# Up projection of a hybrid decoder step: products paired within each token half, six weight pairs in plain form for the first half, norms cut into small steps

## The chip, the cores and the metric

The kernel runs on one core of a Trainium2 chip. The metric is the device time of one execution in microseconds (us). TensorE (PE in the profile) multiplies matrices, VectorE (DVE), ScalarE (ACT) and GpSimd (POOL) work element by element, SyncE (SP) starts transfers between HBM and the on-chip memory SBUF. A product lands in one of eight PSUM banks, and another engine reads it from there.

## The reference

One layer of a decoder for 1024 prompt tokens and 8 sequences of 4 decode tokens, 1056 tokens in all. Two mixing branches run side by side (attention with a forget gate, and a chunkwise mLSTM); their merged output goes through an output projection, two RMS norms with the residual between, and a squared-ReLU MLP. Cut to what lies behind the mixing:

```python
y  = merged @ w_out                                  # 1024 x 1024
x1 = x + gt_m * rmsnorm(y, g_post_mix)
h  = rmsnorm(x1, g_pre_mlp) * (1 + sc_f) + sh_f
u  = jnp.square(jax.nn.relu(h @ w_up))               # w_up 1024 x 4096
x2 = x1 + gt_f * rmsnorm(u @ w_down, g_post_mlp)     # w_down 4096 x 1024
```

Here `sc`, `sh`, `gt` are vectors of a conditioning input, one for the prompt and one for each decode sequence, so the 32 decode columns need factors of their own. They are the last columns of the second token half.

## The kernel before

Activations lie transposed: 128 features on the partitions, tokens along the row. A feature tile (ft) is 128 features; 1024 features are eight of them. Tokens are cut into two halves of 528 (`th` 0 and 1), each into two chunks of 264 (`TQ`).

Each float32 product is made of three matmuls in a faster format. An operand is split into a high part (a cast on ScalarE, `ph`) and a low part (the rest, by a subtraction, `pl`); hi·hi, hi·lo and lo·hi are summed. `split4` does this for a weight of 128x512 (L1237, L1239): every third subtraction goes to VectorE, the others to GpSimd.

*Output projection* (`wout`). For each token half, feature tile and chunk, 24 matmuls go to one of three PSUM banks named `g` (L1386 to L1388). VectorE copies the bank out (L1391), ScalarE squares it, GpSimd adds up the squares (L1397).

*Norms* (`norms(th)`). A generator that is carried on at fixed places. It turns the sums of squares into a scale (`rstd`, L1266 to L1268: small matmuls on TensorE, one step on VectorE, one on GpSimd), spreads it over the partitions by small matmuls (L1279) and, for all eight feature tiles, scales (L1290), adds the residual (L1349), sums squares anew (L1355); then a second `rstd`, a second scaling and a shift on ScalarE (L1365). It has four places to pause. `NORM_AT` lists at which tiles of the second half's output projection a piece of the first half's norm is issued; `NORM2_AT` does it for the second half's norm during the first products of the up projection.

*Up projection*. Weights are taken in pairs of feature tiles, sixteen pairs. Each pair is a 2x2 block product in seven products for eight (Winograd's form). The two block rows of the activations are feature tiles 0-3 and 4-7; the two block columns are the token halves 0 and 1. So the operands (`T1` to `T4`, sums and differences, made and split into hi and lo by `operands`, L1414 to L1426) need both halves. While the second half's norm runs, `first_two` does the two of the seven products that need the first half alone for six pairs (`PRE`), and writes one of them to HBM (`d_s`) for later; ScalarE and VectorE empty its banks (L1463, L1467). After that `operands()` is issued in one go, then `pair` sixteen times, with weight sums `S` on VectorE (L1475 to L1478). Products go to banks named g, s, t and o. Results are squared-ReLU'd on ScalarE (L1449, L1450) and written to HBM (`d_u`).

*Down projection*. Eight blocks `j` of four feature tiles of u. `load_u` (L1563 to L1565) reads them back from HBM and splits them; it stands behind the last pair. There are eight buffers of each part, so two blocks are loaded ahead. Each block multiplies with 32 pieces of w_down (loaded as `raw`, L1230, in three buffers) and adds to accumulators. In the tail come the last norm, transposes and the output's transfers; their tiles use the same eight buffers.

The order on every engine comes from the order in which the program issues instructions, and a scheduler of the framework that works with modelled times. `after(last.ins)` ties a piece to the place behind a given matmul. Every engine runs its own list in order.

Of the kernel before, what the change touches and what calls it, by code (L numbers as in the profile page):

```python
# [18 lines left out]
P = 128  # L19
# [50 lines left out]
def hybrid_kernel(ctx: ExitStack, tc: tile.TileContext, ins, outs):  # L70
# [1112 lines left out]
    ms2 = ExitStack()  # L1183
    mgp = ms2.enter_context(tc.tile_pool(name="mg", bufs=1, reuse_waits="tile", side="right"))
# [9 lines left out]
    MG = [(tl(mgp, [P, 8, TQ], F32R, "X", 8), tl(mgp, [P, 8, TQ], F32R, "X", 8)) for _ in CQ]  # L1194
# [54 lines left out]
    d_s = tl(dr, [PRE, P, TH], F32, "d_s")  # L1249
# [86 lines left out]

    def norms(th):
# [20 lines left out]
        yield  # L1358
# [3 lines left out]
        for ft in range(8):  # L1362
            y = Y(th, ft)
            scaled(y, r2, a_f, ft, m, TH)
            act.activation(y[:, :m], y[:, :m], AF.Identity, bias=sh_f[:, ft, 0:1])  # L1365
            if m < TH:
                per_seq(y, y, sh_f, ft, m, TH, ALU.add)
            if th == 0 and ft % 4 == 3:
                part(ft // 4, Q[0][ft // 4], qp, mgp)
        yield  # L1370

    xTs, turns = {}, {}
    chain = iter(())
    for th in range(2):
        a = th * TH
        Q.append([xs(qp, F32) for _ in range(2)])
        ssq = ssqs[th] = sums(npl, TH)
        for fp in range(4):
            wr = raw_w(w_out, 0, 8, fp * 2 * P, 2 * P)
            for ft in (2 * fp, 2 * fp + 1):  # L1380
                pieces = [split4(wr[:, 4 * kh:4 * kh + 4, (ft % 2) * P:(ft % 2 + 1) * P]) for kh in range(2)]
                for si, (a_, b_) in enumerate(CQ[2 * th:2 * th + 2]):
                    o = bank("g")[:, :TQ]
# [14 lines left out]
                    with after(last.ins):  # L1398
                        if (ft, si) in NORM_AT:
                            next(chain, None)  # L1400
                        if si and ft in XT_AT:
                            if th not in turns:
                                xTs[th] = [xs(mgp if th else qp, F32) for _ in range(2)]
                                turns[th] = turn_x(th)
                            next(turns[th], None)
        for _ in chain:
            pass
        for _ in turns[th]:
            pass
        chain = norms(th)  # L1410
    _mark(nc, "up")


    def operands():  # L1414

        (B11, B21), (B12, B22) = Q
        t3 = xs(qp, F32)
        pool.tensor_tensor(t3, B22, B12, ALU.subtract)
        dve.tensor_tensor(B12, B12, B11, ALU.subtract)
        dve.tensor_tensor(B11, B22, B12, ALU.subtract)  # L1420
        dve.tensor_tensor(B21, B21, B11, ALU.subtract)
# [6 lines left out]
    bank_n = [0]

    def bank8(which="gggsstto"):  # L1430

        bank_n[0] += 1
        return bank(which[bank_n[0] % len(which)])

    SUB = ((0, TQ), (TQ, TH))

    def product(accs_, w, x, first):

        wh, wl = w
        for (s0, s1), acc in zip(SUB, accs_):  # L1440
            o = acc[:, :TQ]
            for k in range(4):
                pe.matmul(o, wh[:, k], hi[x][:, k, s0:s1], start=first and k == 0, stop=False, skip_group_check=True)  # L1443
                pe.matmul(o, wh[:, k], lo[x][:, k, s0:s1], start=False, stop=False, skip_group_check=True)  # L1444
                last = pe.matmul(o, wl[:, k], hi[x][:, k, s0:s1], start=False, stop=k == 3, skip_group_check=True)  # L1445
        return last.ins

    def u_out(c, ft, th):
        act.activation(c, c, AF.Relu)  # L1449
        act.activation(c, c, AF.Square)  # L1450
        sp.dma_start(d_u[ft, :, th * TH:(th + 1) * TH], c)

    def first_two(i, n_):

        wr = raw_w(w_up, 0, 8, 2 * i * P, P)
        A11, A12 = split4(wr[:, 0:4]), split4(wr[:, 4:8])
        ab, bb = [bank8("gggtt") for _ in SUB], [bank8("gggtt") for _ in SUB]
        s = tl(npl, [P, TH], F32, "n", 8)
        c11 = tl(npl, [P, TH], F32, "n", 8)
        last = product(ab, A11, 0, True)  # L1460
        step(last, 2 * n_)
        for (s0, s1), acc in zip(SUB, ab):
            act.copy(s[:, s0:s1], acc[:, :TQ])  # L1463
        last = product(bb, A12, 1, True)
        step(last, 2 * n_ + 1)
        for (s0, s1), acc in zip(SUB, bb):
            dve.tensor_tensor(c11[:, s0:s1], acc[:, :TQ], s[:, s0:s1], ALU.add)  # L1467
        u_out(c11, 2 * i, 0)
        sp.dma_start(d_s[n_], s)

    def pair(i, pre):
# [7 lines left out]
        ab = [bank8() for _ in SUB]  # L1479
        tiles = {}  # L1480
        if pre:
            s = tl(npl, [P, TH], F32, "n", 8)
            sp.dma_start(s, d_s[i])

        def read(what):

            for n_, ((s0, s1), acc) in enumerate(zip(SUB, ab)):
                t = tl(npl, [P, TQ], F32, "v", 4)
                tiles[what, n_] = t
                if pre:  # L1490
                    dve.tensor_tensor(t, acc[:, :TQ], s[:, s0:s1], ALU.add)
                else:
                    act.copy(t, acc[:, :TQ])

        def add(c, what, bb):
            for n_, ((s0, s1), acc) in enumerate(zip(SUB, bb)):
                dve.tensor_tensor(c[:, s0:s1], acc[:, :TQ], tiles[what, n_], ALU.add)

        quad = lambda: tl(npl, [P, TH], F32, "n", 8)
        if not pre:  # L1500
            product(ab, split4(a11), 0, True)
            read("M1")
            bb = [bank8() for _ in SUB]
            product(bb, split4(a12), 1, True)
            c11 = quad()
            add(c11, "M1", bb)
            u_out(c11, 2 * i, 0)
# [5 lines left out]
        read("U3")
        c22 = quad()
        add(c22, "U3", db)
        u_out(c22, 2 * i + 1, 1)
        product(ab, split4(a22), "T4", False)
        c21 = quad()
        for (s0, s1), acc in zip(SUB, ab):
            if pre:  # L1520
                dve.tensor_tensor(c21[:, s0:s1], acc[:, :TQ], s[:, s0:s1], ALU.add)
            else:
                act.copy(c21[:, s0:s1], acc[:, :TQ])
# [6 lines left out]
    def step(last, at):  # L1530
        if at in NORM2_AT:
            with after(last):
                next(chain, None)
# [178 lines left out]
```

## Time and profile before

| | us |
|---|---|
| median of 3 runs | 1930.47 (1926.7 to 1931.01) |
| the profiled execution | 1938.06 |
| its span, first to last instruction | 1936.4 |
| TensorE busy | 1835.9 (95%) |
| VectorE, ScalarE, GpSimd busy | 933.3, 847.0, 498.4 |

The stages that the change touches begin at 1083.0 us of the span (second half of the output projection), 1158.9 (up projection) and 1527.9 (down projection, up to the tail at 1907.9). Matmuls overlap in the trace: one of 264 columns shows 0.28 us, while the next starts 0.12 later. The distance of the starts is what counts.

### The profile page before, as it was taken

To read this page: it belongs to the slowest core of one execution; us is meant where nothing else is said; L and a number is where in the kernel's file an instruction comes from. 1 tells how busy PE (TensorE), PEld (TensorE's weight loads), DVE (VectorE), ACT (ScalarE), POOL (GpSimd) and SP (SyncE) were. 2 spreads that over 40 slices of the span, in tenths; PEclk is the share of its full clock that TensorE was granted. 3 is DMA by queue.
4 is the path that set the end of the run, shared out by engine and by line. 5 is a ranking of instruction groups with operands and counts; after the bars stand their busy time and mean duration, and the time that the engine had idled before them with its cause. 6 is when DMAs were issued, how large, how long until landed. Compare 5 with 4: busy or idle time off the path is not lost.

```text
span 1936.4 us, 31063 instructions
## 1 busy us (share of the span) xinstructions
PE 1835.9 (95%) x12353; PEld 1727.2 (89%) x12353; DVE 933.3 (48%) x1951; ACT 847.0 (44%) x1509; POOL 498.4 (26%) x436
## 2 busy tenths in 40 slices
PE   6899999999999999999998976799999899999998
PEld 3889789898888999989898976799999799999997
DVE  3654545554445565544463446853332324343536
ACT  4646545566555444433123454545555532121212
POOL 3200010000233121101155554322223423222213
PEclk9999989999999999999999988899999899999999
DMA  8321432123556222263234324244333422222213
GB/s 269 77 68 60 142 84 78 45 82 96 175 171 212 88 55 63 70 201 114 66 96 156 123 82 148 95 141 131 95 98 119 173 89 89 95 105 89 89 42 138
DMA packets 182600, 213.37 MB, mean 110 GB/s; under 512 B 14132, under 2 KB 142704, under 8 KB 182456
## 3 DMA queue, kind: packets, MB, share of 16 engines
q1 hardware_dynamic: 177368, 194.43, 31.4%
q0 software_dynamic: 4864, 16.91, 2.6%
q8 instruction: 97, 1.59, 0.3%
q14 instruction: 47, 0.39, 0.1%
q10 hardware_dynamic: 224, 0.06, 0.0%
HBM read 166.08 MB, written 45.29 MB: 109 GB/s over the span
## 4 chain that ended last, share of the span: by engine, by line
PE 87%; DVE 4%; DMA 4%; issue 1%; ACT 1%; POOL 1%; SPq 1%; DVEq 0%; POOLq 0%; ACTq 0%
PE ps_g L408 17%; PE ps_g L410 17%; PE ps_g L409 17%; PE ps_g L1444 2%; PE ps_g L1443 2%; PE ps_g L1445 2%; PE ps_s L684 2%; PE ps_t L709 2%; PE ps_g L1386 2%; PE ps_g L1387 2%; PE ps_g L1388 2%; PE ps_t L1444 1%; PE ps_t L1445 1%; PE ps_t L1443 1%; PE ps_s L681 1%
## 5 line engine op out<-in xcount | busy, mean ns | idle before, releaser
L408 PE MATMUL ps_g<-Xh,wh 128*128 128x352 f32 (+1 forms) x1176 | 394.3, 336 | 1.2 <-ACT wh L269 1.0
L410 PE MATMUL ps_g<-Xh,wl 128*128 128x352 f32 (+1 forms) x1176 | 390.9, 334 | 0.0
L409 PE MATMUL ps_g<-Xl,wh 128*128 128x352 f32 (+1 forms) x1080 | 356.5, 330 | 0.6 <-DVE Xl L351 0.6
L408 PEld LDWEIGHTS ps_g<-Xh,wh 128*128 128x128 f32 (+1 forms) x1176 | 223.4, 190 | 7.4 <-issue 3.0
L410 PEld LDWEIGHTS ps_g<-Xh,wl 128*128 128x128 f32 (+1 forms) x1176 | 222.4, 189 | 6.2 <-issue 4.5
L408 PE MATMUL ps_g<-uh,ph 128*128 128x352 f32 x672 | 217.7, 325 | 8.1 <-ACT uh L1564 8.1
L409 PE MATMUL ps_g<-ul,ph 128*128 128x352 f32 x672 | 216.8, 323 | 1.3 <-POOL ul L1565 1.3
L410 PE MATMUL ps_g<-uh,pl 128*128 128x352 f32 x672 | 216.4, 322 | 0.0
L409 PEld LDWEIGHTS ps_g<-Xl,wh 128*128 128x128 f32 (+1 forms) x1080 | 203.9, 189 | 6.8 <-issue 3.9
L1239 POOL TENSOR_TENSOR pl<-raw,ph 128x512 fp32r<-128x512 f32 x92 | 126.9, 1381 | 280.5 <-ACT ph L1237 275.0
L1237 ACT CAST ph<-raw 128x512 fp32r<-128x512 f32 x136 | 84.0, 621 | 263.1 <-PE ps_g L409 178.6
L270 POOL TENSOR_TENSOR wl<-wr,wh 128x1024 fp32r<-128x1024 f32 x26 | 63.2, 2429 | 442.7 <-ACT wh L269 293.9
L1580 DVE TENSOR_TENSOR acc<-acc,ps_g 128x352 f32<-128x352 f32 x144 | 74.0, 519 | 163.3 <-PE ps_g L410 163.3
L408 PEld LDWEIGHTS ps_g<-uh,ph 128*128 128x128 f32 x672 | 126.8, 189 | 9.3 <-ACT uh L1564 8.3
L409 PEld LDWEIGHTS ps_g<-ul,ph 128*128 128x128 f32 x672 | 127.1, 189 | 1.7 <-POOL ul L1565 1.7
L410 PEld LDWEIGHTS ps_g<-uh,pl 128*128 128x128 f32 x672 | 126.8, 189 | 0.0
L1443 PE MATMUL ps_g<-X,ph 128*128 128x264 f32 x376 | 108.4, 289 | 12.1 <-ACT X L1311 12.1
L1444 PE MATMUL ps_g<-X,ph 128*128 128x264 f32 x376 | 108.8, 290 | 0.5 <-DVE X L1312 0.5
L1445 PE MATMUL ps_g<-X,pl 128*128 128x264 f32 x376 | 108.2, 288 | 0.0
L1386 PE MATMUL ps_g<-X,ph 128*128 128x264 f32 x256 | 77.4, 302 | 19.2 <-DVE X L1391 13.3
L1239 POOL TENSOR_TENSOR pl<-S,ph 128x512 fp32r<-128x512 f32 x42 | 57.4, 1368 | 141.1 <-ACT ph L1237 141.1
L269 ACT CAST wh<-wr 128x1024 fp32r<-128x1024 f32 x52 | 54.5, 1047 | 75.7 <-PE ps_g L409 55.0
(618 smaller groups left out, 4496.2 us busy)
## 6 DMA issues: line engine op xcount, KB each, us to landing
wr<-in_w_in SPq DMA_DIRECT2D x44, 512.0 KB
d_u<-n SPq DMA_DIRECT2D x64, 264.0 KB
ul<-d_u SPq DMA_DIRECT2D x32, 528.0 KB
wr<-in_w_ada SPq DMA_DIRECT2D x32, 512.0 KB
raw<-in_w_up SPq DMA_DIRECT2D x16, 1024.0 KB
raw<-in_w_down SPq DMA_DIRECT2D x16, 1024.0 KB
d_sg<-sgo SPq DMA_DIRECT2D x60, 176.0 KB
raw<-in_w_out SPq DMA_DIRECT2D x8, 1024.0 KB
```

Of the source, the lines that this page charges most:

```text
L269: act.copy(wh, wr)
L270: (dve if lo_turn[0] % 2 else pool).tensor_sub(wl, wr, f(wh))
L408: pe.matmul(o, wh[:, k], rh(k, a, b), start=(k == 0), stop=False)
L409: pe.matmul(o, wh[:, k], rl(k, a, b), start=False, stop=False)
L410: last = pe.matmul(o, wl[:, k], rh(k, a, b), start=False, stop=(k == nk - 1))
L1237: act.copy(h_, src)
L1239: (dve if turn[0] % 3 == 0 else pool).tensor_sub(l_, src, f(h_))
L1386: pe.matmul(o, wh[:, kk], mg_h(k, a_, b_), start=(k == 0), stop=False)
L1443: pe.matmul(o, wh[:, k], hi[x][:, k, s0:s1], start=first and k == 0, stop=False, skip_group_check=True)
L1444: pe.matmul(o, wh[:, k], lo[x][:, k, s0:s1], start=False, stop=False, skip_group_check=True)
L1445: last = pe.matmul(o, wl[:, k], hi[x][:, k, s0:s1], start=False, stop=k == 3, skip_group_check=True)
L1580: dve.tensor_tensor(accs[a // 352](ft), accs[a // 352](ft), o, ALU.add)
```

## The change

- The 2x2 block product now lies within one token half: the block columns are the half's two chunks of 264 tokens. Each half has operands of its own (`operands(th)`), of 128x1056, in named places (`AT`).
- The first six pairs are done for the first half alone in plain form (`plain`: eight block products, 96 matmuls a pair), then pairs 6 to 15 for both halves (168 each), then pairs 0 to 5 for the second half alone (84 each). `d_s` is gone.
- `norms` pauses after each feature tile and `operands` after each one or two operands: 46 steps, spread by two tables (`AT_OUT` with 21 over the 16 tiles of the second half's output projection, `AT_UP` with 25 over the 24 tiles of the plain products). The second half's residual tiles (`x_tile(1)`) move from the output projection into the plain products. Decode columns of four feature tiles are scaled by one instruction.
- The output projection and the plain products use five banks in turn (`g`, `g`, `t`, `g`, `t`). In `plain` ScalarE empties the bank with its ReLU, and all splits' subtractions go to GpSimd.
- In a pair, one of the two squared ReLUs is one step on VectorE.
- The down projection takes the blocks in the order 3 to 7, 0 to 2. Its first activations are loaded and split during the second half's pairs, into places `R0` to `R3`; those of later blocks have four buffers a block in alternation, and the tail's tiles have four for eight.

```diff
-NORM_AT = ((0, 0), (0, 1), (2, 1), (3, 1), (4, 0), (4, 1))
-NORM2_AT = (0, 1, 4, 5, 6, 7)
+AT_OUT = (1, 1, 2, 1, 2, 1, 1, 0, 1, 2, 2, 2, 2, 1, 1, 1)
+AT_UP = ((3, 1), (2, 2), *((0, n) for n in (1, 1, 2, 1, ...)))
...
-    def split4(src):
+    def split4(src, every=3):
...
-        (dve if turn[0] % 3 == 0 else pool).tensor_sub(l_, src, f(h_))
+        (dve if turn[0] % every == 0 else pool).tensor_sub(l_, src, f(h_))
...
         for ft in range(8):
             y = Y(th, ft)
-            scaled(y, r, gt_m, ft, m, TH)
+            if ft % 4 == 0 and m < TH:
+                scaled_s(Q[th][ft // 4], r, gt_m, ft // 4, m)
+            scaled_p(y, r, gt_m, ft, m)
             (pool if ft % 2 else dve).tensor_tensor(y, y, xT[ft // 4][:, ft % 4], ALU.add)
...
-        yield
+            yield
         rt = rstd(ssq2, TH)
...
+    def blocks(th):
+        return [Q[th][k][:, :, c * TQ:(c + 1) * TQ] for k in range(2) for c in range(2)]
+    def operands(th):
+        B11, B12, B21, B22 = blocks(th)
+        part(th, "B11", B11, at["B11"])
+        part(th, "B21", B21, at["B21"])
         yield
+        if th == 0:
+            part(th, "B12", B12, at["B12"])
+            part(th, "B22", B22, at["B22"])
+            yield
+        pool.tensor_tensor(t3, B22, B12, ALU.subtract)
+        dve.tensor_tensor(B12, B12, B11, ALU.subtract)
+        dve.tensor_tensor(B11, B22, B12, ALU.subtract)
+        dve.tensor_tensor(B21, B21, B11, ALU.subtract)
+        yield
+        part(th, "T2", B11, at["T2"])
+        part(th, "T1", B12, at["T1"])
+        yield
...
-                    o = bank("g")[:, :TQ]
+                    o = bank8("ggtgt")[:, :TQ]
...
-                        if (ft, si) in NORM_AT:
-                            next(chain, None)
+                        if th:
+                            steps(AT_OUT[2 * ft + si])
...
+    def plain(i, anchors):
+        for s_ in range(2):
+            pieces = [split4(wr[:, 4 * kh:4 * kh + 4, s_ * P:(s_ + 1) * P], every=99) for kh in range(2)]
+            for n_ in range(2):
+                o = bank8("ggtgt")[:, :TQ]
+                for k in range(8):
+                    (wh, wl), x, kk = pieces[k // 4], (0, f"B{k // 4 + 1}{n_ + 1}"), k % 4
+                    pe.matmul(o, wh[:, kk], hi[x][:, kk], start=(k == 0), stop=False)
+                    pe.matmul(o, wh[:, kk], lo[x][:, kk], start=False, stop=False)
+                    last = pe.matmul(o, wl[:, kk], hi[x][:, kk], start=False, stop=(k == 7))
+                act.activation(c[:, n_ * TQ:(n_ + 1) * TQ], o, AF.Relu)
...
+                with after(last.ins):
+                    at = next(anchors)
+                    for _ in range(at[0]):
+                        x_tile(1)
+                    steps(at[1])
...
+            dve.scalar_tensor_tensor(c, c, 0.0, c, ALU.max, ALU.mult)
...
+    chain = itertools.chain(chain, norms(1), operands(1))
     for i in range(PRE):
-        first_two(i, i)
+        plain(i, anchors)
     for _ in chain:
         pass
-    operands()
-    for i in range(FF // (2 * P)):
-        pair(i, i < PRE)
+    for i in range(PRE, FF // (2 * P)):
+        pair(i, (0, 1))
...
+    JS = [*range((PRE + 1) // 2, NJ), *range((PRE + 1) // 2)]
...
+            if n_ == 0:
+                t = tl(mgp, [P, 2, T], F32R, f"R{i}", 1)
+                ht, lt = t[:, 0], t[:, 1]
+            else:
+                ht, lt = (tl(dnp, [P, T], F32R, x + "ab"[n_ % 2], FC) for x in ("uh", "ul"))
...
+    for i in range(PRE):
+        pair(i, (1,))
+        if i == 1:
+            u_0 = load_u(0)
...
-            yt = tl(dnp, [P, T], F32, "ul", 8)[:, :D]
+            yt = tl(dnp, [P, T], F32, "ula", FC)[:, :D]
```

The order of instructions shows three places. First TensorE in the second half of the output projection, where the norm's second scale is made (L1266 sums, L1279 spreads it, both lines are the same in the two kernels). Before, one product stands between the two:

```order
L1386 MATMUL ps_g_11468<-X_9710,ph_11464 128x264
L1387 MATMUL ps_g_11468<-X_9711,ph_11464 128x264
L1266 MATMUL ps_o_11248<-u_7_91,ssq_11072 128x1 x5
L1388 MATMUL ps_g_11468<-X_9710,pl_11465 128x264
L1279 MATMUL ps_s_11325<-u_4_82,rt_11250 128x128 x4
L1279 MATMUL ps_s_11331<-u_4_82,rt_11250 128x16
L1386 MATMUL ps_g_11497<-X_9712,ph_11460 128x264
```

After (the products are L1458 to L1460), 34 stand between:

```order
L1460 MATMUL ps_g_11446<-R_1852_9712,pl_11406 128x264
L1266 MATMUL ps_o_11352<-u_7_91,ssq_11071 128x1 x5
L1458 MATMUL ps_g_11446<-R_1852_9712,ph_11405 128x264
...
L1460 MATMUL ps_g_11446<-R_1852_9712,pl_11410 128x264
L1458 MATMUL ps_t_11489<-R_1850_9710,ph_11481 128x264
...
L1458 MATMUL ps_t_11489<-R_1850_9710,ph_11485 128x264
L1279 MATMUL ps_s_11392<-u_4_82,rt_11354 128x128 x4
L1279 MATMUL ps_s_11398<-u_4_82,rt_11354 128x16
L1459 MATMUL ps_t_11489<-R_1851_9711,ph_11485 128x264
```

The sums stand at nearly the same place of TensorE's list (row 6167 before, 6171 after). What moved is L1279, from two rows behind them to 35 behind.

Second, TensorE where the last matmuls of the output projection (operands `X_11354`, `R_1852`) end and the next products begin. Before, this is the start of the seven products (`X_12285` is the first activation operand; six banks are opened by one product each):

```order
L1445 MATMUL ps_t_12221<-X_11354,pl_12215 128x264
L1443 MATMUL ps_g_12315<-X_12285,ph_12319 128x264
L1443 MATMUL ps_g_12316<-X_12285,ph_12319 128x264
L1443 MATMUL ps_t_12497<-X_12285,ph_12501 128x264
L1443 MATMUL ps_t_12498<-X_12285,ph_12501 128x264
L1443 MATMUL ps_s_12351<-X_12289,ph_12353 128x264
L1443 MATMUL ps_s_12352<-X_12289,ph_12353 128x264
L1444 MATMUL ps_g_12315<-X_12286,ph_12319 128x264
L1445 MATMUL ps_g_12315<-X_12285,pl_12320 128x264
```

After, the plain products follow directly (`R_2104`, `L_2112` are operands of feature tiles 0-3, `R_2105`, `R_2113` of 4-7):

```order
L1460 MATMUL ps_t_11600<-R_1852_9712,pl_11562 128x264
L1513 MATMUL ps_g_11645<-R_2104_11551,ph_11637 128x264
L1513 MATMUL ps_g_11814<-R_2104_11551,ph_11806 128x264
L1513 MATMUL ps_g_11857<-L_2112_11594,ph_11806 128x264
L1514 MATMUL ps_g_11645<-R_2104_11551,ph_11637 128x264
L1515 MATMUL ps_g_11645<-R_2104_11551,pl_11638 128x264
...
L1515 MATMUL ps_g_11857<-L_2112_11594,pl_11807 128x264
L1513 MATMUL ps_g_11645<-R_2105_11554,ph_11641 128x264
L1513 MATMUL ps_g_11814<-R_2105_11554,ph_11810 128x264
L1513 MATMUL ps_g_11857<-R_2113_11597,ph_11810 128x264
L1514 MATMUL ps_g_11645<-R_2105_11554,ph_11641 128x264
```

Three banks are opened, and 36 products need the first two operands alone before one of the others is read.

Third, SyncE's queue at the start of the down projection (`raw` are weights, `ul`, `R`, `ulb`, `ula` activations of later blocks, `d_u`<-`n` results of up). Before:

```order
L1230 DMA raw_16095<-in_w_down 128x4x512
L1451 DMA d_u_10365<-n_15703 128x528
L1230 DMA raw_16301<-in_w_down 128x4x512
L1451 DMA d_u_10365<-n_15871 128x528
L1563 DMA ul_15889<-d_u_10365 128x1056
L1563 DMA ul_15894<-d_u_10365 128x1056
...
L1563 DMA ul_16281<-d_u_10365 128x1056
L1563 DMA ul_16286<-d_u_10365 128x1056
...
L1230 DMA raw_16487<-in_w_down 128x4x512
L1230 DMA raw_16693<-in_w_down 128x4x512
```

After:

```order
L1593 DMA R_2665_15376<-d_u_10364 128x1056
L1501 DMA d_u_10364<-n_14612 128x528
...
L1593 DMA R_2666_15380<-d_u_10364 128x1056
...
L1501 DMA d_u_10364<-n_15828 128x528
L1231 DMA raw_16552<-in_w_down 128x4x512
L1231 DMA raw_16758<-in_w_down 128x4x512
L1593 DMA ulb_16347<-d_u_10364 128x1056
L1593 DMA ulb_16352<-d_u_10364 128x1056
...
L1593 DMA ula_16739<-d_u_10364 128x1056
...
L1231 DMA raw_16944<-in_w_down 128x4x512
```

The first block's loads (`R_2665` on) moved up among the results of up; the second block's (`ulb`) and the third's now stand behind the fifth weight load.

## Rows read from the trace of the kernel before

**Rows 1.** The profile's first section: busy us, share of the span, instructions

```profile
PE 1835.9 (95%) x12353; PEld 1727.2 (89%) x12353; DVE 933.3 (48%) x1951; ACT 847.0 (44%) x1509; POOL 498.4 (26%) x436
```

**Rows 2.** Waits of TensorE, 1000 to 1940: us, times, longest

```profile
PE ps_g L1386 <- DVE X L1391: 13.3, 2, 9.3
PE ps_t L1443 <- DVE n L1467: 13.2, 1, 13.2
PE ps_g L1443 <- ACT X L1311: 12.1, 1, 12.1
PE ps_g L408 <- ACT uh L1564: 8.1, 1, 8.1
...
PE ps_s L1279 <- POOL rt L1268: 4.1, 2, 2.8
```

**Rows 3.** Busy us by stage and engine; granted clock, DMA share last

```profile
1083.00:1158.90 75.90, 61.30 (x465) 60.38 (x465) 40.89 (x49) 35.18 (x64) 42.72 (x36) 0.87 0.29 93
1158.90:1240.00 81.10, 51.91 (x365) 50.25 (x365) 58.28 (x98) 38.12 (x64) 34.38 (x20) 0.79 0.37 123
1240.00:1527.90 287.90, 287.90 (x2367) 287.90 (x2365) 112.02 (x209) 153.76 (x293) 85.14 (x66) 1.00 0.36 114
1527.90:1545.00 17.10, 7.78 (x32) 7.11 (x31) 7.04 (x5) 10.31 (x12) 9.12 (x6) 0.70 0.86 327
1545.00:1907.90 362.90, 362.85 (x2284) 361.72 (x2283) 147.26 (x232) 83.69 (x132) 102.95 (x66) 1.00 0.24 84
```

**Rows 4.** Timeline of TensorE: start, us, engine, line, operation, [idle before <-releaser]

```profile
1102.78 0.28 PE L1388 MATMUL ps_g<-X,pl 128*128 128x264 f32 x1
1107.07 0.56 PE L1386 MATMUL ps_g<-X,ph 128*128 128x264 f32 x1 [4.00 <-DVE X L1391]
1107.43 0.42 PE L1387 MATMUL ps_g<-X,ph 128*128 128x264 f32 x1
1107.65 0.42 PE L1388 MATMUL ps_g<-X,pl 128*128 128x264 f32 x1
...
1113.10 0.29 PE L1386 MATMUL ps_g<-X,ph 128*128 128x264 f32 x1
...
1536.18 1.25 PE L408 MATMUL ps_g<-uh,ph 128*128 128x352 f32 x3 [8.06 <-ACT uh L1564]
```

**Rows 5.** Groups of instructions, 1080 to 1545: count, busy us, mean ns, idle before

```profile
L1239 POOL TENSOR_TENSOR pl<-raw,ph 128x512 fp32r<-128x512 f32 x44 | 58.8, 1337 | 92.9 <-ACT ph L1237 87.4 <-PE ps_g L1445 5.1 <-PE ps_t L1333 0.2
...
L1290 DVE SCALAR_TENSOR_TENSOR X<-X,mod,n 128x528 f32<-128x528 f32 x16 | 16.3, 1091 | 5.0 <-ACT n L1280 5.0
L1312 DVE TENSOR_TENSOR X<-X,X 128x2112 fp32r<-128x2112 f32 x7 | 16.2, 2349 | 1.1 <-ACT X L1311 1.1
L1397 POOL TENSOR_TENSOR ssq<-ssq,v 128x264 f32<-128x264 f32 x16 | 15.0, 949 | 23.5 <-ACT v L1396 23.5
L1349 POOL TENSOR_TENSOR X<-X,X 128x528 f32<-128x528 f32 x8 | 15.0, 1882 | 6.4 <-DVE X L1286 4.8 <-DVE X L1290 1.3
...
L1349 DVE TENSOR_TENSOR X<-X,X 128x528 f32<-128x528 f32 x8 | 7.4, 956 | 0.0
```

**Rows 6.** Timeline of VectorE around the first half's norm

```profile
1095.18 10.78 DVE L1290 SCALAR_TENSOR_TENSOR X<-X,mod,n 128x528 f32<-128x528 f32 x8 [1.75 <-ACT n L1280]
...
1122.22 1.78 DVE L1355 TENSOR_TENSOR ssq<-ssq,n 128x528 f32<-128x528 f32 x1 [1.44 <-POOL ssq L1355]
...
1129.73 5.52 DVE L1290 SCALAR_TENSOR_TENSOR X<-X,mod,n 128x528 f32<-128x528 f32 x8 [3.21 <-ACT n L1280]
```

**Rows 7.** Timeline of GpSimd beside the first group above

```profile
1099.49 1.75 POOL L1239 TENSOR_TENSOR pl<-raw,ph 128x512 fp32r<-128x512 f32 x1
```

**Rows 8.** Timeline of SyncE's queue at the start of the down projection

```profile
1531.17 4.47 SPq L1563 DMA_DIRECT2D ul<-d_u  x8
1554.15 22.63 SPq L1230 DMA_DIRECT2D raw<-in_w_down  x2
```

**Rows 9.** Timeline of ScalarE at the same place

```profile
1535.05 1.07 ACT L1564 CAST uh<-ul 128x1056 fp32r<-128x1056 f32 x1 [4.33 <-DMA ul<-d_u]
```

More of the change, by code (lines that the diff above doesn't have):

```diff
@@ L1 @@
+import itertools
 from contextlib import ExitStack, contextmanager, nullcontext
@@ L1372, in hybrid_kernel, with steps, x_tile @@
+    AT = ({"x": ("L2", "L3"), "y": ("L0", "L1"), "t3": "L2", "B11": "R0", "B21": "R1", "B12": "L6", "B22": "R3",
+           "T1": "R2", "T2": "L3", "T3": "L0", "T4": "L2"},
+          {"x": ("R4", "R5"), "y": ("L4", "L5"), "t3": "R4", "B11": "R6", "B21": "R7", "T2": "L1", "T1": "R5",
+           "T3": "L4", "T4": "R4", "B22": "L6"})
     xTs, turns = {}, {}
     chain = iter(())
+    def steps(n):
+        for _ in range(n):
+            next(chain, None)
+    def x_tile(th):
+        if th not in turns:
+            xTs[th] = [xs(at, F32) for at in AT[th]["x"]]
+            turns[th] = turn_x(th)
+        next(turns[th], None)
@@ L1428, in hybrid_kernel @@
[L1428 to L1435, printed above, removed]
+                        if th:
+                            steps(AT_OUT[2 * ft + si])
+                        elif si and ft in XT_AT:
+                            x_tile(0)
+        if th == 0:
+            for _ in turns[0]:
+                pass
+            chain = itertools.chain(norms(0), operands(0))
+    _mark(nc, "up")
     def product(accs_, w, x, first):
@@ L1446, in product @@
[L1446 to L1469, printed above, removed]
@@ L1472, in pair @@
+    def pair(i, hs):
         wr = raw_w(w_up, 0, 8, 2 * i * P, 2 * P)
@@ L1478, in pair @@
         dve.tensor_tensor(S[3], a12, S[1], ALU.subtract)
-        ab = [bank8() for _ in SUB]
+        banks = lambda: {h: bank8() for h in hs}
         tiles = {}
[L1481 to L1507, printed above, removed]
@@ L1508, in pair, with read, add @@
-        product(ab, split4(S[1]), "T2", pre)
-        read("U2")
-        db = [bank8() for _ in SUB]
+        c1, c2 = {h: quad() for h in hs}, {h: quad() for h in hs}
+        one_, two_ = slice(0, TQ), slice(TQ, TH)
+        def read(what, accs_):
+            for h in hs:
+                t = tiles[what, h] = tl(npl, [P, TQ], F32, "v", 4)
+                act.copy(t, accs_[h][:, :TQ])
+        def add(c, cols, what, accs_):
+            for h in hs:
+                dve.tensor_tensor(c[h][:, cols], accs_[h][:, :TQ], tiles[what, h], ALU.add)
@@ L1511, in pair @@
+        ab = banks()
+        product(ab, split4(a11), "B11", True)
+        read("M1", ab)
+        bb = banks()
+        product(bb, split4(a12), "B21", True)
+        add(c1, one_, "M1", bb)
+        product(ab, split4(S[1]), "T2", False)
+        read("U2", ab)
+        db = banks()
         product(db, split4(S[0]), "T1", True)
         product(ab, split4(S[2]), "T3", False)
[L1513 to L1516, printed above, removed]
+        read("U3", ab)
@@ L1517, in pair @@
+        add(c2, two_, "U3", db)
         product(ab, split4(a22), "T4", False)
[L1518 to L1523, printed above, removed]
-        u_out(c21, 2 * i + 1, 0)
-        product(db, split4(S[3]), "B22", False)
-        c12 = quad()
-        add(c12, "U2", db)
-        u_out(c12, 2 * i, 1)
[L1530 to L1533, printed above, removed]
+        for h in hs:
+            act.copy(c2[h][:, one_], ab[h][:, :TQ])
+            u_out(c2[h], 2 * i + 1, h, "D")
```

135 lines of the change are left out of this document (75 added, 60 removed).

## The prediction

> **What bounds the kernel now.** I read the page's first section: TensorE is busy for 95% of the span [rows 1], so time can be won only from its idle time, its clock or its number of matmuls. Next, what TensorE waited for [rows 2], then busy time by stage [rows 3], since the change touches only the end: the second half of the output projection (from 1083.0 us), the up projection (1158.9) and the start of the down projection (1527.9). In the three disturbed stages TensorE is idle for 75.9 - 61.3 = 14.6, 81.1 - 51.9 = 29.2 and 17.1 - 7.8 = 9.3, together 53.1 us; in the long middle of the up projection it is never idle [rows 3]. The waits give the names: PSUM copies of the output projection (13.3 in two), the first products of up (13.2), the operands of the seven products (12.1), the down projection's first activations (8.1), the second norm's scale (4.1) [rows 2].
>
> Behind a stall there is a second loss. [...] The granted clock of the three stages, 0.87, 0.79 and 0.70 against 1.00 [rows 3], tells the same. Six stalls in these stages are longer than 2 us; at 2.8 each, a little under the one shown, they lose 17 us.
>
> So 53 + 17 = 70 us lie in the stretch as loss. That is the ceiling, and it isn't all free.
>
> **What the change costs in work.** The matmul pitch at full clock is 287.9 / 2367 = 0.1216 us [rows 3]. Before, sixteen pairs take 168 matmuls each: 2688. After, six plain ones take 96, ten full pairs 168 and six half pairs 84: 576 + 1680 + 504 = 2760. That is 72 more: +8.8 us. If every stall went, the gain would be 70 - 8.8 = 61 us.
>
> **What is moved, and what is late next.**
>
> 1. Output projection, copies. DVE still issues eight scale steps in a row, 10.8 us when they meet GpSimd [rows 6]; a PSUM copy queued behind them waits as before. With three banks TensorE gets 3 x 24 x 0.1216 = 8.8 us ahead, with five 14.6. So this wait goes, and what hides it is the two more banks. The chain does not: from DVE's first scale step at 1095.18 to the end of the last sum of squares, 1122.22 + 1.78 = 1124.0 [rows 6], it runs 28.8 us, ending 41 after the half began (1083.0). TensorE, no longer held by the copies, comes to the second norm's sums after some 270 matmuls and the transposes, 35 to 36 us in. It then waits: 0 if splits on GpSimd fall kindly, 8 if the chain is drawn out; I take 5, the difference to the 41 of the rows. The scale itself (4.1 in rows 2) now comes 34 matmuls (4.1 us) after the sums and is hidden.
>
> 2. Start of up. After the scale DVE needs eight scale steps (5.5 alone [rows 6]) and two copies, ScalarE a shift and a cast per tile, DVE a low part of 1.2 for each operand (half of the 2.35 for 128x2112 [rows 5]): some 12 to 15 us to the second operand. TensorE has 82 matmuls of wout left, 10 us, then 36 that need only the first operands. The old wait of 13.2 came from DVE's evacuation behind the second half's norm; ScalarE does it now, and the norm stands later. I take 5.5, from 0 (all hidden by those 10 + 4.4 us) to 10 (nearest: the 12.1 that the operands cost before, halved in size and with some cover).
>
> 3. Second half's norm and operands. These gave the 13.2 and the 12.1 in rows 2. They now lie in small steps beside 576 plain matmuls, 70 us, which need nothing of them. Bounds 0 and 8 (the scale's 4.1 twice); I take 2.5.
>
> 4. Half pairs. TensorE needs 84 x 0.1216 = 10.2 us for one, while each still asks for all seven splits and four weight sums. GpSimd: 4.67 splits x 1.34 = 6.2; DVE: four weight sums, 2.33 splits and one output step, about 0.69 each like a scale step alone of nearly the same size [rows 6], together 5.1. Neither is full alone. Were they to exclude each other the sum is 11.3 as met, some 9.7 by the durations alone: -0.5 to +1.1 us a pair. Four activations for down come into the same stretch, two on each engine, 10 us. So 0 to 14; I take 4, as the work ahead of the half pairs is idle enough to run ahead (DVE 112 and POOL 85 of 288 us [rows 3]).
>
> 5. Start of down. The old 9.3 us of idle begins with loads issued at 1531.17 and cast at 1535.05 [rows 8, 9]; the changed kernel has these four loads while the half pairs run, so it goes. Late next is the second block: its loads stand on SP behind the fifth weight load, which waits for a buffer. Before, that one was issued at 1554.15 + 22.6 = 1576.8 [rows 8] at the latest, 40 us after the block began (1536.18 [rows 4]). A block lasts 362.9 / 8 = 45.4 us [rows 3]; issue, landing 3.9, cast and subtraction come to some 45 to 48. 0 to 5; I take 1.5.
>
> 6. Tail. Four buffers instead of eight make ScalarE's copies wait for output transfers. The nearest row is the 3.9 us of a transfer [rows 8, 9]; nothing is gained there, since no other work of the tail changes. 0 to 3.9; I take 0.5.
>
> 7. The clock. Each stall over some 3 us costs up to another 3.0 [rows 4]. 0 to 10; I take 4.
>
> Sum of losses: 5 + 5.5 + 2.5 + 4 + 1.5 + 0.5 + 4 = 23. Net: 61 - 23 = 38 us. The profiled execution took 1938.06 (span 1936.4), so 1900; the median of the runs shown is 7.6 below it, so **1892**.
>
> [...] Eight scale steps of DVE took 10.78 us while GpSimd had work on SBUF, 5.52 while it had none; GpSimd's subtraction beside them took 1.75, in the mean of this part 1.34 [rows 5 to 7]. [...]
>
> [...]
>
> **The rivals.**
>
> [...]
> - *Nearly all hidden.* The small steps fit, the queues run ahead, the five banks cover the rest; losses 4 to 12, so 1874 to 1882, mid 1878. For it: TensorE is never idle in the 288 us where DVE and GpSimd work as steadily [rows 3]. Against: term 1's chain, 41 us to TensorE's 35.
> [...]
>
> **How the numbers follow.** Forecast (losses 12 to 33: 1882 to 1902) 0.57; nearly all hidden 0.17; shared access 0.19; slower 0.05; a balance at no change 0.02. About 0.2%, 4 us, is what a measurement of this kernel can tell from no change. The first three cases are all faster, bar the edge of the third: faster 0.92, same 0.03, slower 0.05. The range takes in "nearly all hidden" and the better half of "shared access": 1873 to 1914.
>
> **What would show it.** Right: up holds 2760 product matmuls at 0.12 us; the waits on the PSUM copies in wout, on the evacuation (13.2) and on down's first cast (8.1) are gone; what is left stands at the second norm's sums, at the first products of up and in the half pairs, each under 10 us; the granted clock of 1083 to 1240 is above 0.9. [...] Wrong: a wait of over 10 us at the start of up, at the second block of down or in the tail, or a stretch of half clock through the half pairs.

## The result and the profile after

The changed kernel takes 1917.5 us, the kernel before 1931.1 (medians of 19 runs each): ratio 0.993, 95% interval 0.991 to 0.995, so 9 to 17 us faster. Forecast were 1892 and a range of 1873 to 1914: the sign was right, the gain a third of the 38 us.

Single runs of the changed kernel lie between 1907 and 1929 us. A good part of that is chance in code that the change leaves alone: up to the output projection's first product the profiled execution of before spent 70 us at a granted clock of 0.5 and that of after 41, and before came to it 12.8 us later. (In the traces of all kernels of this document it is 38 to 73 us.) So the two traces are compared from the output projection's first product on: 906.5 us before, 895.9 after, 10.6 less.

First the waits of TensorE in the changed kernel from 1000 us on (total us, times, longest), to be held against [rows 2]:

```profile
PE ps_g L1458 <- ACT ph L1238: 5.8, 1, 5.8
PE ps_o L1266 <- DVE ssq L1372: 5.2, 1, 5.2
PE ps_t L1513 <- ACT n L1516: 3.9, 2, 2.4
PE ps_s L1491 <- DVE pl L1240: 3.1, 1, 3.1
PE ps_g L1514 <- DVE R L1313: 2.7, 1, 2.7
PE ps_g L1489 <- ACT v L1543: 2.6, 1, 2.6
PE ps_g L409 <- ACT acc L1624: 2.6, 1, 2.6
PE ps_g L409 <- ACT uhb L1594: 1.9, 1, 1.9
PE ps_g L1489 <- ACT ph L1238: 1.7, 3, 0.9
PE ps_g L410 <- POOL ulb L1595: 1.7, 1, 1.7
```

The waits of 13.3, 13.2, 12.1 and 8.1 us are gone (the 5.8 is the output projection's start, which the change doesn't touch). Eight stalls of 1.7 to 5.2 us stand in their place. By stage (columns as in [rows 3]; second half of the output projection, plain products, full pairs, half pairs, first block of down, the rest of down):

```profile
1070.00:1129.30 59.30, 54.10 (x424) 53.62 (x423) 36.50 (x45) 26.43 (x51) 41.60 (x35) 0.94 0.33 107
1129.30:1220.50 91.20, 84.62 (x659) 83.34 (x658) 61.33 (x58) 51.70 (x100) 62.44 (x37) 0.94 0.40 131
1220.50:1421.00 200.50, 197.88 (x1614) 197.68 (x1613) 92.40 (x144) 92.41 (x190) 64.38 (x47) 0.99 0.35 111
1421.00:1508.00 87.00, 79.59 (x611) 78.45 (x610) 48.93 (x67) 47.29 (x95) 45.68 (x35) 0.96 0.42 143
1508.00:1565.00 57.00, 52.77 (x298) 51.82 (x299) 13.02 (x9) 22.33 (x39) 18.98 (x9) 0.91 0.34 120
1565.00:1893.00 328.00, 326.86 (x2038) 325.93 (x2037) 147.47 (x241) 66.50 (x101) 92.58 (x63) 1.00 0.24 84
```

No stage is bad, but only the last is free of idle time.

The starts of all matmuls in the trace give a full account from the output projection's first product to the end (us). A matmul's full-clock cost is the mean distance to the next one, away from stalls; what it takes above that at a granted clock of 0.5 is the clock's loss; a distance of over 0.45 us is counted as idle; "not told apart" is what is left over.

| | before | after | change | forecast |
|---|---|---|---|---|
| 264-column products, 3456 and 3528 | 420.4 | 429.3 | +8.9 | +8.8 |
| 352-column products of down, 2303 seen | 367.5 | 373.0 | +5.5 | 0 |
| small matmuls | 22.3 | 22.4 | 0 | 0 |
| idle | 56.5 | 29.7 | -26.8 | -34.6 |
| lost at the lower clock | 16.6 | 16.7 | 0 | -13 |
| not told apart | 4.8 | 4.8 | 0 | |
| tail behind the last down product | 18.4 | 20.0 | +1.6 | +0.5 |
| sum | 906.5 | 895.9 | -10.6 | -38 |

So three things ate the gain: the clock (13), idle time (8), and a slower pace of the down projection (5.5), which the forecast had not at all. One trace stands for each kernel here. Four kernels below have the same stalls up to the down projection (three with a pad of 32 or 96 bytes, one with copies on VectorE); counted alike, they lost 0.4 to 2.3 us less at the lower clock, so 2 us in that row say little.

### The profile page after: what moved, and what is told of

Read it like the earlier page. It is cut to its first block, busy times and chain, and to the rows that moved or that the text cites. A ratio compares the mean times of both kernels' runs of the same rounds, so it can differ in the third digit from the quotient of the medians.

```text
span 1913.0 us, 31223 instructions
## 1 busy us (share of the span) xinstructions
PE 1839.1 (96%) x12425; PEld 1733.9 (91%) x12425; DVE 960.2 (50%) x1904; ACT 829.5 (43%) x1513; POOL 542.2 (28%) x461
## 4 chain that ended last, share of the span: by engine, by line
PE 86%; DVE 5%; DMA 4%; issue 1%; ACT 1%; SPq 1%; POOL 1%; DVEq 0%; ACTq 0%; POOLq 0%
PE ps_g L409 17%; PE ps_g L411 17%; PE ps_g L410 17%; PE ps_s L685 2%; PE ps_g L1489 2%; PE ps_g L1491 2%; PE ps_g L1490 2%; PE ps_t L710 2%; PE ps_s L682 1%; PE ps_s L1491 1%; PE ps_s L1489 1%; PE ps_s L1490 1%; PE ps_t L1489 1%; PE ps_t L1490 1%; PE ps_t L1491 1%
## 5 line engine op out<-in xcount | busy, mean ns | idle before, releaser
L410 PE MATMUL ps_g<-Xl,wh 128*128 128x352 f32 (+1 forms) x1080 | 355.9, 330 | 1.1 <-DVE Xl L352 0.9
L1240 POOL TENSOR_TENSOR pl<-raw,ph 128x512 fp32r<-128x512 f32 x116 | 170.4, 1473 | 304.4 <-ACT ph L1238 286.3
L410 PEld LDWEIGHTS ps_g<-Xl,wh 128*128 128x128 f32 (+1 forms) x1080 | 203.4, 188 | 7.2 <-issue 3.9
L409 PE MATMUL ps_g<-uhb,ph 128*128 128x352 f32 x288 | 93.8, 328 | 2.6 <-ACT uhb L1594 1.9
L410 PE MATMUL ps_g<-ulb,ph 128*128 128x352 f32 x288 | 94.2, 327 | 1.7 <-POOL ulb L1595 1.7
L411 PE MATMUL ps_g<-uhb,pl 128*128 128x352 f32 x288 | 94.4, 328 | 0.0
L409 PE MATMUL ps_g<-uha,ph 128*128 128x352 f32 x288 | 93.5, 325 | 0.0
L411 PE MATMUL ps_g<-uha,pl 128*128 128x352 f32 x288 | 93.3, 324 | 0.0
L410 PE MATMUL ps_g<-ula,ph 128*128 128x352 f32 x288 | 93.0, 323 | 0.0
L686 DVE CUSTOM_DVE_ANT_0 Pt<-ps_s,nF 128x384 f32<-128x384 f32 (+4 forms) x96 | 51.8, 554 | 64.0 <-PE ps_t L710 39.5
L693 ACT ACTIVATE Pt<-Pt,nm 128x128 f32<-128x128 f32 (+3 forms) x64 | 49.7, 777 | 31.8 <-DVE nm L691 20.7
L712 ACT CAST PT<-ps_t 128x512 fp32r<-128x512 f32 (+1 forms) x80 | 40.5, 545 | 52.9 <-PE ps_t L710 52.1
```

The lines of the kernel that those rows point to most:

```text
L409: pe.matmul(o, wh[:, k], rh(k, a, b), start=(k == 0), stop=False)
L410: pe.matmul(o, wh[:, k], rl(k, a, b), start=False, stop=False)
L411: last = pe.matmul(o, wl[:, k], rh(k, a, b), start=False, stop=(k == nk - 1))
L686: dve.tensor_tensor_reduce(Pt[:, k0:k1], s_, nF[:, k0:k1], 1.0, -3.0e38, ALU.add, ALU.max, mx[:, pi:pi + 1])
L1240: (dve if turn[0] % every == 0 else pool).tensor_sub(l_, src, f(h_))
```

## The experiments

**The pace of the down projection.** In steady state its 352-column matmuls started 0.1596 us apart before, 0.1619 after; in 100 us of it (window, span, busy and count of TensorE first) before and after:

```profile
1610.00:1710.00 100.00, 100.00 (x630) 99.99 (x629) 39.77 (x63) 18.96 (x26) 28.22 (x16) 1.00 0.25 86
```

```profile
1610.00:1710.00 100.00, 100.00 (x620) 100.00 (x619) 43.96 (x64) 21.00 (x28) 30.13 (x18) 1.00 0.25 86
```

TensorE is full in both, at a granted clock of 1.00, with 630 and 620 records. The buffers of the activations moved: in the compiled programs they begin at multiples of 128 bytes of a partition before, 96 bytes behind one after. The input projection's operands lie 96 behind in both kernels, and there the pace is 0.162 in both.

```diff
+            tl(ctx.enter_context(tc.tile_pool(name="pad", bufs=1, side="right")), [P, 8], F32, "pad", 1)
             dnp = ctx.enter_context(tc.tile_pool(name="dnp", ..., side="right"))
```

> The changed kernel with 32 bytes left free ahead of the down projection's activation buffers, so that they begin at a multiple of 64 bytes, as they did in the kernel before, and not 32 bytes behind one. Theory A (start address): the matmuls of 352 columns in blocks 2 to 8 come 0.1595 us apart as before the change, not 0.1619; 2016 of them, so 4.8 us less than the changed kernel, some 1912 to 1913 against 1917.5. Theory B (the pace comes from something else: the side of the memory on which the buffers lie, the transfers, another chip): the pace stays at 0.162 and the time within 2 us of 1917.5.

The distance fell to 0.1604. The time: ratio 0.995 to before (0.992 to 0.998), which can't be told from the changed kernel's 0.993; 3 us lie inside the spread.

> The kernel before with the same buffers moved the other way, from a multiple of 64 bytes to 32 behind one; nothing else moves on TensorE. Theory A (start address): the pace of the down projection's matmuls goes from 0.1595 to 0.162 us, 2304 x 0.0024 = 5.5 us slower than before, some 1936. Theory B: no change of the pace, within 2 us of 1931.

The pad went ahead of the left-side buffers. The distance went to 0.1600 only, ratio 1.000 (0.996 to 1.004): as put there, theory A fell. Not every start off the 64 bytes is slow.

> The changed kernel with the 32 bytes left free ahead of everything on that side of the memory, so that the input projection's operands and the up projection's begin at multiples of 64 bytes too. Theory A: besides the 5.5 us of the down projection the 3300 matmuls of 352 columns in the input projection go from 0.1623 to 0.1595 us, another 8 to 9 us: 14 us less than the changed kernel, some 1903 to 1904; the 264-column products, whose rows are 16.5 times 64 bytes, change little. Theory B: within 2 us of 1917.5.

Input projection 0.1602 for 0.1621, down 0.1603; ratio 0.986 (0.981 to 0.990).

The same pad with 24 for 8 elements:

> The changed kernel with 96 bytes left free on that side of the memory, so that the 352-column operands of the input and the down projection begin at multiples of 128 bytes. With 32 bytes (64 beyond a multiple of 128) the pace was 0.1602 and 0.1603 us; in the kernel before, whose down projection begins at multiples of 128, 0.1596; 32 beyond, 0.1600; 96 beyond, 0.162. Theory A1 (the pace goes by the start within 128 bytes): 0.1596 us in both stages, 5500 matmuls x 0.0024 = 13 us less than the changed kernel, some 1904. Theory A2 (only the multiple of 64 counts): 0.1602 as with 32 bytes, 10 us less. Theory B (the pace is the chip's or the side's): 0.162.

Down 0.1593, input projection 0.1600; ratio 0.988 (0.984 to 0.993). The same 100 us window of down:

```profile
1610.00:1710.00 100.00, 100.00 (x630) 100.00 (x630) 41.87 (x63) 22.70 (x30) 31.34 (x18) 1.00 0.30 108
```

630 again. So in these runs the pace went with the start address: 0.1593 to 0.1596 in down for starts at multiples of 128 bytes, 0.1600 for 32 behind, 0.1603 for 64, 0.1619 for 96. The input projection, with 0.1600 at multiples of 128, follows it less; why is open.

**Who holds up the norms.**

```diff
         h_ = tl(w2p, [P, 4, P], F32R, "ph", NPC)
-        l_ = tl(w2p, [P, 4, P], F32R, "pl", NPC)
         act.copy(h_, src)
         turn[0] += 1
+        if every == 99:
+            return h_, h_
+        l_ = tl(w2p, [P, 4, P], F32R, "pl", NPC)
```

> The changed kernel with the low parts of the plain pairs' weights left out: GpSimd's 24 subtractions there are not done, TensorE multiplies the high part in their place, so its work is the same. Theory C (GpSimd and VectorE hold each other up on SBUF, so the second half's norm drags and the PSUM copies queued behind it on ScalarE come late): VectorE's scale steps in the plain products fall from 1.7 to about 0.7 us, the two waits of TensorE there (2.4 and 1.5) go, and with the clock that they cost 5 to 8 us are won, some 1910. Theory D (it is the chain's own length and order): the waits stay, under 2 us of difference.

The two waits in the plain products fell from 3.9 to 1.2 us together, that at the first full pair (2.6) vanished; idle 29.7 to 23.7, clock 16.7 to 13.7. The ratio, 0.989 (0.984 to 0.993), can't be told from the changed kernel's. The scale steps of 496 columns, first in the changed kernel, then here (count, busy, mean ns, idle before):

```profile
L1344 DVE SCALAR_TENSOR_TENSOR L<-L,mod,n 128x496 f32<-128x496 f32 x16 | 17.1, 1120 | 5.4 <-ACT n L1280 5.4
```

```profile
L1346 DVE SCALAR_TENSOR_TENSOR L<-L,mod,n 128x496 f32<-128x496 f32 x16 | 14.1, 930 | 10.7 <-ACT n L1282 10.7
```

The means hide the pattern: of the 16 steps six took some 1.8 us in the changed kernel and three here, the others 0.73, so GpSimd's residual adds still meet three. The timelines (start, us, engine and line) of VectorE, GpSimd and ScalarE at that place of the changed kernel show it:

```profile
1165.33 5.13 DVE L1344 SCALAR_TENSOR_TENSOR L<-L,mod,n 128x496 f32<-128x496 f32 x3
1170.39 1.78 DVE L1366 TENSOR_TENSOR L<-L,R 128x528 f32<-128x528 f32 x1
1172.09 5.18 DVE L1344 SCALAR_TENSOR_TENSOR L<-L,mod,n 128x496 f32<-128x496 f32 x3
```

```profile
1171.56 1.78 POOL L1366 TENSOR_TENSOR L<-L,R 128x528 f32<-128x528 f32 x1
1173.30 1.72 POOL L1240 TENSOR_TENSOR pl<-raw,ph 128x512 fp32r<-128x512 f32 x1
1174.97 1.76 POOL L1366 TENSOR_TENSOR L<-L,R 128x528 f32<-128x528 f32 x1
```

```profile
1177.92 1.71 ACT L1371 ACTIVATE n<-L 128x528 f32<-128x528 f32 x3 [6.08 <-DVE L L1366]
1179.54 0.37 ACT L1516 ACTIVATE n<-ps_t 128x264 f32<-128x264 f32 x1
```

Both engines go at one step per 1.72 us, turn by turn, and the squares on ScalarE wait 6.1 us for them, with the PSUM copy (L1516) behind them that TensorE waits for. Theory C holds here for some 6 us of idle time in the trace; of the 3 of clock 2 lie within what the same stalls vary by.

> The changed kernel with the low parts of the weights in the second half of the output projection left out: 16 subtractions, 11 of them on GpSimd, are not done, TensorE multiplies the high part in their place. Theory C (GpSimd and VectorE hold each other up, and this draws out the first half's norm): the eight scale steps take about 6 to 8 us instead of 10.8, the wait for the second norm's sums (5.2) falls below 2, and so does the wait for the first operands (2.7); with the clock 7 to 10 us less, some 1909. Theory D (the chain's own length, 28.8 us before, of which only a part is waiting): the 5.2 falls by 2 at most.

The edit is the same with `every == 4` for the second half. The 5.2 fell to 2.4, in part a new wait of 1.8 on GpSimd took the place of the 2.7; idle 29.7 to 27.3, ratio 0.989 (0.984 to 0.993). Between the theories: without the 16 subtractions the eight scale steps take 8.8 us for 10.8 and the chain from them to the last sum 23.2 for 28.0, but its own length remains.

**What the five banks hide.**

```diff
-                    o = bank8("ggtgt")[:, :TQ]
+                    o = bank("g")[:, :TQ]
... (the same in plain)
```

> The changed kernel with three PSUM banks instead of five in the output projection and the plain products. Theory G (as the prediction had it, five banks are what hides the PSUM copies): waits on the copies come back, at least 4 us in the output projection and several of 2 to 5 us in the plain products where the copies stand behind a norm step, 10 to 20 us slower than the changed kernel, some 1930. Theory H (the small steps of the norms suffice): within 4 us of 1917.

Ratio 0.992 (0.988 to 0.995): no slower. Theory G fell. Its waits, the first ones:

```profile
PE ps_g L1458 <- ACT ph L1238: 5.9, 1, 5.9
PE ps_g L1458 <- DVE L L1463: 4.0, 1, 4.0
PE ps_g L1514 <- DVE R L1313: 3.6, 2, 2.8
PE ps_s L1491 <- DVE pl L1240: 3.1, 1, 3.1
PE ps_g L1513 <- ACT n L1516: 2.7, 2, 1.9
PE ps_g L409 <- ACT acc L1624: 2.6, 1, 2.6
PE ps_o L1266 <- DVE ssq L1372: 2.2, 1, 2.2
```

The wait on the copy is back with 4.0 us, and the wait at the second norm's sums fell by 3.0. So in these two kernels TensorE waits for one chain, and the banks only choose where.

**The start of the second block of down.** In the changed kernel, SyncE's loads and ScalarE's casts:

```profile
1540.54 2.03 SPq L1593 DMA_DIRECT2D ulb<-d_u  x4
```

```profile
1550.42 0.62 ACT L1238 CAST ph<-raw 128x512 fp32r<-128x512 f32 x1 [1.39 <-PE ps_g L410]
1550.94 0.45 ACT L1624 COPY acc<-ps_g 128x352 f32<-128x352 f32 x1
1551.29 3.99 ACT L1594 CAST uhb<-ulb 128x1056 fp32r<-128x1056 f32 x4
```

The loads were issued 10.7 us ahead of the first cast; a like load took 3.9 [rows 8, 9].

```diff
-                    act.copy(accs[a // 352](ft), o)
+                    dve.tensor_copy(accs[a // 352](ft), o)
```

> The changed kernel with the first block's PSUM copies in the down projection on VectorE instead of ScalarE. Theory E (the second block's activations landed in time, but their casts stand behind the first block's last copy on ScalarE): the casts begin some 5 us earlier, TensorE's waits there (1.9, 1.7 and 0.6) go, and perhaps the 2.6 at the first block's start; with the clock 5 to 8 us less than the changed kernel, some 1911. Theory F, that of the prediction (the loads come late, behind the fifth weight load): the waits stay, within 2 us of 1917.

The wait at the first block's start fell from 2.6 to 1.3, those at the second came to 1.6 and 2.0, as before; ratio 0.991 (0.988 to 0.994). The casts still stand behind a weight cast:

```profile
1544.62 0.62 ACT L1238 CAST ph<-raw 128x512 fp32r<-128x512 f32 x1 [5.23 <-PE ps_g L410]
1545.14 3.99 ACT L1594 CAST uhb<-ulb 128x1056 fp32r<-128x1056 f32 x4
```

That one waits 5.2 us for a matmul (L410), which gives the buffer back only near the block's end. The loads had been issued at 1534.74. So neither theory: ScalarE's queue it is, but the weight cast in it, not the copy.

```diff
-            if n_ == 0:
-                t = tl(mgp, [P, 2, T], F32R, f"R{i}", 1)
+            if n_ < 2:
+                t = tl(mgp, [P, 2, T], F32R, f"R{4 * n_ + i}", 1)
...
             u_0 = load_u(0)
+    u_1 = load_u(1)
...
```

> The changed kernel with the second block's activations of the down projection loaded and split ahead of the first block's products, into the places that the pairs leave free; the third block's stand where they did. Theory E2 (in the changed kernel the loads land 5 us early, but the casts stand behind a weight cast or the last PSUM copy on ScalarE): the waits at the second block (1.9, 1.7, 0.6) go, 4.5 us with 1 to 2 of the clock; if the third block's loads now come behind the seventh weight load, a wait of 2 to 8 us comes there instead. Theory F (nothing to be had, the engines are full there): a wait of the same size at the first block.

Ratio 1.000 (0.998 to 1.003), slower than the changed kernel. The waits from 1490 us on:

```profile
PE ps_g L409 <- ACT acc L1623: 7.1, 1, 7.1
PE ps_g L410 <- POOL ula L1595: 2.0, 1, 2.0
PE ps_g L409 <- ACT uha L1594: 1.6, 1, 1.6
```

The second block's waits went, and the third block has the very same, in front of a 7.1 at the first block, whose copies now stand behind the early casts.

**What a stall costs in clock.** A wait made on purpose at the start of full pairs:

```diff
+        if hold is not None:
+            act.copy(h_[:, 0, 0:1], hold[:, 0:1])
...
+        held = 7 <= i < 15 and len(hs) == 2
...
+        prev[0] = ab[hs[-1]]
```

`hold` is the bank of the pair before. For the four long waits `held` also asks for an odd pair (`i % 2`), and the bank is that of the pair's last product (`db`).

> The changed kernel with a wait made on purpose at the start of eight of the ten full pairs: the first weight's cast must follow a PSUM read of the pair before. Estimated 1.5 to 3 us of idle TensorE each, 12 to 24 in all. Theory I (each stall costs clock, whatever its length: in the two profiles 6 to 8 stalls of 2 to 13 us lost 16.6 and 16.7 us): another 8 x 1.5 to 2.5 us of slow matmuls, so that the kernel loses nearly twice the idle time, 25 to 40 us. Theory J (the clock's loss goes with the idle time, 0.3 us for each us as in the kernel before): 4 to 7 us beside the idle time, 16 to 31 in all.

> The same with four such waits, each about twice as long (the read is of the pair's last product): estimated 4 to 6 us each, 16 to 24 in all. Theory I: four times 1.5 to 2.5, 6 to 10 us of slow matmuls, half of what the eight short ones lose for a like idle time. Theory J: 5 to 7, the same as the eight.

The eight came out in pieces of 0.4 to 1.1 us, 12 us in these pairs and 14.7 in all; the clock's loss stayed at 16.6. (Some 1.5 us of it lie in these pairs; in exchange the 2.7 us wait at the start of the plain products had shrunk to 0.7 at the longest.) The four came out as pairs of 2 to 3 and 0.5 to 1.5 us, 16.0 more idle time, and the clock's loss rose to 25.4: 2.2 for each. So a place with 1.5 us of idle time cost the clock little, one with 4.0 us 2.2; whether the longer piece or the sum counts isn't told apart. Ratios 1.003 (1.000 to 1.006) and 1.013 (1.010 to 1.016). The ten full pairs in the changed kernel, with eight, with four (granted clock third from the end):

```profile
1232.50:1432.50 200.00, 200.00 (x1644) 200.00 (x1644) 86.38 (x141) 88.89 (x185) 65.86 (x48) 1.00 0.34 106
```

```profile
1232.00:1446.00 214.00, 205.93 (x1633) 201.35 (x1632) 107.28 (x138) 90.06 (x194) 73.14 (x48) 0.99 0.29 98
```

```profile
1240.00:1465.00 225.00, 211.55 (x1642) 208.52 (x1641) 91.25 (x140) 89.84 (x190) 65.92 (x48) 0.95 0.29 94
```

Both theories fell in part: theory I gives the price of the four (6 to 10), not of the eight; J the price of neither. In the rows of the two kernels the price doesn't go by length either. The stall of 13.2 us before [rows 2] was followed by 3.0 us at a granted clock of 0.50. The clock had fallen while TensorE still stood idle, 0.56 in the mean of the stall's last 12 us, so most of the slow time cost nothing:

```profile
1173.00:1185.00 12.00, 0.00 (x0) 0.00 (x0) 11.90 (x27) 3.53 (x7) 7.33 (x4) 0.56 0.12 47
```

This stall of 3.1 us, in the half pairs of the changed kernel, was followed by 5.7 at 0.50:

```profile
1448.35 0.28 PE L1490 MATMUL ps_s<-R,ph 128*128 128x264 f32 x1
1451.73 0.59 PE L1491 MATMUL ps_s<-R,pl 128*128 128x264 f32 x1 [3.10 <-DVE pl L1240]
1452.12 0.42 PE L1489 MATMUL ps_s<-R,ph 128*128 128x264 f32 x1
...
1457.18 0.37 PE L1490 MATMUL ps_s<-R,ph 128*128 128x264 f32 x1
1457.38 0.29 PE L1491 MATMUL ps_s<-R,pl 128*128 128x264 f32 x1
```

And the same stall of 3.1 us, in the kernel with three banks, by none. The 10 us from the last matmul ahead of it, in the changed kernel and there:

```profile
1448.35:1458.35 10.00, 6.90 (x36) 6.69 (x35) 5.75 (x9) 3.49 (x7) 2.79 (x3) 0.66 0.34 124
```

```profile
1445.70:1455.70 10.00, 6.90 (x57) 6.69 (x56) 7.35 (x11) 4.74 (x9) 4.85 (x4) 1.00 0.35 124
```

Over the twelve traces that have this stall the matmuls behind it lost 0.5 to 2.9 us, 1.9 in the mean. So 2 us is a mean price; for a single stall it varies from run to run, and what decides it stays open.

**The 96 bytes and the three banks together.**

> The changed kernel with both edits that cost nothing: 96 bytes left free and three PSUM banks. If they add up (13 us by the pace of the 352-column products, 3 by the banks in the profiled execution): some 1902, and faster than either kernel. If the banks were noise: 1905 as with the 96 bytes alone.

1901.4 us against 1923.8 of before on the same chip, ratio 0.988 (0.986 to 0.991). Against the changed kernel's 0.993 that is half a per cent, some 9 us more; from the output projection's first product on 889.4 us for 895.9. The two intervals (0.991 to 0.995 there) just meet. It cannot be told from the 96 bytes alone, nor from the 32 bytes ahead of everything, whose 0.981 to 0.990 is clear of the changed kernel.

## Why the prediction was wrong

*The ceiling was right.* 53 us idle and 17 at the lower clock were forecast as the loss of the stretch, 8.8 us as the price of 72 more matmuls; the account has 56.5 (1.3 of it in the tail's first step), 16.6 and 8.9.

*Term 7, the clock, failed: 4 us forecast, 16.7 measured.* This is half of the miss. The prediction saw that each stall has a loss behind it and then let the loss shrink with the idle time. But eight stalls of 1.7 to 5.2 us cost the clock what six of 3 to 13 did: in the 13.2 us stall the slow clock fell for the most part into the idle time, behind the short ones onto matmuls. The experiment with made stalls gives 2.2 us for each place of 2 to 3 us and a shorter piece, and some 1.5 for all eight places of smaller pieces. Cutting a long stall into pieces of some 3 us brought the idle time down here and left the clock's loss where it was. Chance doesn't explain the miss: the four kernels with the same stalls lost 14 to 16. (The ceiling's 2.8 us a stall and the 3.0 of this term go back to the stall at 1103 [rows 4]: behind it 27 matmuls took 6.03 us, 0.22 apart, at a granted clock of 0.51, so 6.03 - 27 x 0.1216 = 2.75 us were lost.) Nor did it take a stall of over some 3 us: behind the one of 2.7 us at the start of the plain products the granted clock was 0.50 for another 6.2 us, from 1137.1 to 1143.3.

*Terms 1 to 3 were right in sum, not in reason.* Forecast 5 + 5.5 + 2.5 = 13.0; the account has 5.4, 3.0 and 4.2, together 12.6. The wait at the second norm's sums came where and as large as forecast, since the chain of 28.8 us [rows 6] is nearly the same, 28.0: the eight scale steps took 10.8 us again. But that the five banks hide the PSUM copies "and so this wait goes" was no gain: with three banks the stage is as fast. In the plain products the wait isn't the scale's but a PSUM copy on ScalarE behind the norm's squares, drawn out by the turn-by-turn pace of VectorE and GpSimd.

*Term 4 was half of what came.* The half pairs have 5.5 us, forecast 4; the 2.8 at the first full pair, whose operands come late when GpSimd's subtractions are there (with those left out it was gone), had no term.

*Term 5 had the wrong mechanism and 1.5 for 7.6 us.* The loads were in time. 2.7 came at the first block, whose copies stand on ScalarE among the last pairs' work; 4.9 at the second, whose casts stand behind a weight cast that waits for a buffer. (The weights of down have two raw buffers, not three as stated above.)

*The down projection's pace had no term.* It was priced as unchanged work, since neither its matmuls nor their number changed. Its buffers moved, 96 bytes behind a multiple of 128, and 2304 matmuls took 0.0023 us more each: 5.5 us. The tail (term 6) took 1.6 us more, forecast 0.5.

*The rivals.* "Shared access", whose better half ends the range at 1914, was nearest in time. That VectorE and GpSimd, by holding each other up, would set the pace of the stretch in TensorE's place was the author's estimate; no run shows it. The runs show that the two went by turns between 1165 and 1177 us of the changed kernel, one step per 1.72 us each, against 0.69 for a scale step alone [rows 6]. Yet terms 1 to 3 lost 12.6 us there, forecast 13.0, and leaving out GpSimd's subtractions took 6 us of idle time in the plain products and 2.4 in the output projection. Term 4's 9.7 us for a half pair "by the durations alone" was too low as well: with 0.69 for each of VectorE's 7.33 steps it leaves 1.0 us for each of GpSimd's subtractions, and in the trace of before none of these took under 1.25 us.

*The base.* The profiled execution of before was 7.6 us above its median, and taking that off was right: the median of 19 runs is 1931.1. That the clock ahead of the stretch made the difference is likely, not shown: single runs of before on one chip have a granted clock of 0.976 at 1914.7 us and of 0.964 at 1935.0.

## What to carry to other kernels

When long stalls are cut into short ones, count the stalls that remain and not only their sum: those of 2 to 5 us had some 2 us of slow clock each in the mean here, anything from 0 to 3 in a single case. Work that a change doesn't touch can still change its pace if its buffers move (0.1596 to 0.1619 us a matmul here); compare the matmuls' distance in an undisturbed stretch, and try a pad of 32 to 96 bytes before anything cleverer. A wait that is taken away at one place on an in-order chain can come back at the next, as with the three banks and with the early second block; ask which chain ends last, and what stands ahead of the needed instruction in its engine's queue.

## What was not expected of the hardware

The pace of the 352-column float32 matmuls went with where their moving operand begins: 0.1593 to 0.1596 us at multiples of 128 bytes and 0.1619 at 96 behind, in the down projection, with TensorE full and at a granted clock of 1.00. The input projection, which the change left alone, ran at the slow pace in both kernels; the pad of 96 bytes took it from 0.1621 to 0.1600, 3456 matmuls by 0.0021, 7 us.
